# Groups of four matrices, 32-bit transposes and row-shifting copies in a batched matrix product

## The chip, the cores and the metric

The kernel runs on one NeuronCore of a Trainium2 chip. A core has a matrix engine (TensorE, in profiles PE, with its weight loads as PEld), a vector engine (VectorE, DVE), a scalar engine (ScalarE, ACT), a general engine (GpSimd, POOL) and a synchronisation engine (SyncE, SP), which here only issues transfers. Sixteen DMA engines move data between the device memory and SBUF, the on-chip memory of 128 partitions. PSUM is the small memory into which TensorE writes. Each engine works through its own instructions in order and waits on semaphores for the others. The metric is the device time of one execution, in microseconds.

## The reference

```python
b1, b2, m, k, n = 8, 16, 256, 512, 384
# x: (8, 16, 256, 512) float32, weight: (8, 16, 512, 384) float32
def reference(x, weight):
    return np.matmul(x, weight).astype(np.float32)
```

These are 128 independent products of a 256 x 512 matrix with a 512 x 384 matrix. All inputs and outputs are fp32; 168 MB are read and 50 MB written.

## The kernel before

TensorE contracts over partitions, so both operands must have the index k on the partitions. The weights have it there when they are loaded: partition kp holds the four rows k = 4 kp + ko (ko from 0 to 3) of one matrix, 6 KB in one run. x has its rows on the partitions and must be transposed on the chip.

The work is done in groups of two matrices (63 groups), and at the end two groups of one. For a pair, `load_x` (L58, its transfer issued at L60) loads 512 rows of x, four neighbouring rows to a partition (R = 4), so that each partition reads one run of 8 KB. `load_w` (L65, transfer L67) loads each weight matrix by itself.

`transpose_x` (L70) casts x to bf16 on DVE (L77). Then TensorE transposes: for each of the four rows of a partition and each ko, the 128 x 128 block of the columns ko, ko + 4, ... is transposed against an identity (L82), eight blocks to a PSUM tile `pt` of bf16, and DVE copies the tile into `x_t` (L86). The weights are cast to bf16 on DVE (L110).

Since 64 partitions of x belong to the first matrix of the pair and 64 to the second, the output of a matmul (L125) is only 64 rows wide: it takes 64 columns of `x_t` as its stationary operand and 384 columns of the weights as moving operand, and writes partitions 0 to 63 or 64 to 127 of a PSUM tile `po`. Four matmuls (ko) accumulate one result; those of the two matrices alternate. Each `po` holds two rows per partition, and ACT copies it into `out_sb` (L132), 128 partitions x 768 elements. The output has four neighbouring rows to a partition, as x has, so the store (L95) writes runs of 6 KB.

All transfers are issued by SyncE, in the order of the program: the x of a pair, its two weight matrices, then the store of an earlier pair. A store is held back until more than LAG = 4 are waiting. Buffers: `x_pool` 3, `w_pool` 6, `xb_pool` and `xt_pool` 2, `wb_pool` 4, `out_pool` 7, `psum_t` 2 and `psum_o` 3. The tile framework places the waits: a load waits until the cast that read its buffer is over, and a copy into a buffer waits until its last store is over. It also has at most eight transfers under way: each waits for the eighth before it. The instructions of one engine are put into an order by the framework's scheduler, which need not be that of the source.

Of the kernel before, what the change touches and what calls it, by code (L numbers as in the profile page):

```python
# [1 line left out]

# [5 lines left out]


@with_exitstack
def kernel(
    ctx: ExitStack,
    tc: tile.TileContext,
    x: bass.AP,
    weight: bass.AP,
    out: bass.AP,
):
    nc = tc.nc
    P = 128  # L20

    b1, b2, M, K = x.shape
    _, _, _, N = weight.shape
    B = b1 * b2
    KO = K // P

    x_rows = x.rearrange("b1 b2 m k -> (b1 b2 m) k")
    o_rows = out.rearrange("b1 b2 m n -> (b1 b2 m) n")
    w_flat = weight.rearrange("b1 b2 k n -> (b1 b2) k n")

    fp32 = mybir.dt.float32
    bf16 = mybir.dt.bfloat16

    GX = 2
    CX = P // GX
    R = GX * M // P


    groups = [2] * ((B - GX) // 2) + [1] * GX

    LAG = 4

    const = ctx.enter_context(tc.tile_pool(name="const", bufs=1))
    x_pool = ctx.enter_context(tc.tile_pool(name="x_pool", bufs=3))
    xb_pool = ctx.enter_context(tc.tile_pool(name="xb_pool", bufs=2))
    xt_pool = ctx.enter_context(tc.tile_pool(name="xt_pool", bufs=2))
    w_pool = ctx.enter_context(tc.tile_pool(name="w_pool", bufs=6))
    wb_pool = ctx.enter_context(tc.tile_pool(name="wb_pool", bufs=4))  # L50
    out_pool = ctx.enter_context(tc.tile_pool(name="out_pool", bufs=LAG + 3))
    psum_t = ctx.enter_context(tc.tile_pool(name="psum_t", bufs=2, space=bass.MemoryType.PSUM))
    psum_o = ctx.enter_context(tc.tile_pool(name="psum_o", bufs=3, space=bass.MemoryType.PSUM))

    identity = const.tile([P, P], bf16)
    make_identity(nc, identity)

    def load_x(b):  # L58
        x_sb = x_pool.tile([P, R, K], fp32, name="x_sb")
        nc.sync.dma_start(  # L60
            x_sb[:], x_rows[b * M : (b + GX) * M].rearrange("(p r) k -> p r k", r=R)
        )
        return x_sb

    def load_w(b):  # L65
        w_sb = w_pool.tile([P, KO, N], fp32, name="w_sb")
        nc.sync.dma_start(w_sb[:], w_flat[b].rearrange("(kp ko) n -> kp ko n", ko=KO))  # L67
        return w_sb

    def transpose_x(x_sb, RG):  # L70


        H = R // RG
        x_bf = xb_pool.tile([P, R, K], bf16, name="x_bf")
        x_t = xt_pool.tile([P, RG, KO, P, H], bf16, name="x_t")
        for r0 in range(0, R, 4):
            nc.vector.tensor_copy(out=x_bf[:, r0 : r0 + 4], in_=x_sb[:, r0 : r0 + 4])  # L77
            for r in range(r0, r0 + 4, 2):
                pt = psum_t.tile([P, 2, KO, P], bf16, name="pt")
                for rr in range(2):  # L80
                    for ko in range(KO):
                        nc.tensor.transpose(  # L82
                            pt[:, rr, ko, :], x_bf[:, r + rr, ko::KO], identity
                        )
                j = r % RG
                nc.vector.tensor_copy(  # L86
                    out=x_t[:, j : j + 2, :, :, r // RG], in_=pt[:]
                )
        return x_t

    waiting = []

    def store(queue):
        dram, out_sb = waiting.pop(0)
        queue.dma_start(out=dram, in_=out_sb)  # L95

    b = 0
    for n, G in enumerate(groups):
        last = n == len(groups) - 1
        C = P // G  # L100
        RG = G * M // P
        if b % GX == 0:
            x_sb = load_x(b)
        w_sb = [load_w(b + i) for i in range(G)]
        if b % GX == 0:
            x_t = transpose_x(x_sb, RG)
        w_bf = []
        for i in range(G):
            t = wb_pool.tile([P, KO, N], bf16, name="w_bf")
            nc.vector.tensor_copy(out=t[:], in_=w_sb[i][:])  # L110
            w_bf.append(t)
        if last:

            while waiting:
                store(nc.sync)

        out_full = out_pool.tile([P, 2 * M // P, N], fp32, name="out_sb")
        out_sb = out_full[:, :RG]
        for r in range(0, RG, 2):
            po = psum_o.tile([P, 2, 512], fp32, name="po")  # L120
            for rr in range(2):
                for ko in range(KO):
                    for i in range(G):
                        c0 = (b % GX + i) * CX
                        nc.tensor.matmul(  # L125
                            po[i * C : (i + 1) * C, rr, :N],
                            x_t[:, r + rr, ko, c0 : c0 + CX, :],
                            w_bf[i][:, ko, :],
                            start=(ko == 0),
                            stop=(ko == KO - 1),  # L130
                        )
            nc.scalar.copy(out=out_sb[:, r : r + 2, :], in_=po[:, :, :N])  # L132
        waiting.append(
            (
                o_rows[b * M : (b + G) * M].rearrange("(p r) n -> p r n", r=RG),
                out_sb,
            )
        )
        if len(waiting) > LAG or last:
            store(nc.sync)  # L140
        b += G


# [1 line left out]
_INS = ['x', 'weight']  # L145
_OUTS = [((8, 16, 256, 384), 'float32')]


# [23 lines left out]
```

## Time and profile before

| | |
|---|---|
| median of 3 runs | 526.35 us (526.27 to 526.38) |
| profiled execution | 526.34 us, of which its span is 524.1 us |
| HBM read, written | 167.77 MB, 50.33 MB |
| mean rate of the DMA | 417 GB/s |
| mean granted TensorE clock | 0.87 |
| w loads / x loads / stores, median from issue to landing | 16.0 us each |

The span runs from the first to the last recorded event of one execution; the execution's own time is 2.2 us longer. Busy times are sums over an engine's instructions. In the lines on the instruction groups, the numbers after the bar are the total busy time in us and the mean duration of one instruction in ns, and after the second bar the idle time just ahead of these instructions with what ended most of it. In the view of waits, the numbers are the total in us, the count and the longest. In the timeline a line gives the start, the length, the engine, the source line, the operation and the number of instructions merged into it.

### The profile page before, as it was taken

The page shows a single profiled execution, that of the slowest core. Times are in us where ns is not written, and L with a number is a line of the kernel's source. Part 1 is how long each engine was busy: PE and PEld are TensorE (multiplying, and loading weights), DVE is VectorE, ACT ScalarE, POOL GpSimd, SP SyncE. Part 2 cuts the span into 40 slices and gives each one's busy share as a digit, 9 for nine tenths or more (in the row PEclk, how much of TensorE's full clock was granted, in tenths as well). Part 3 has the DMA queues.
Part 4 walks back from the last instruction along what each step waited for, and adds up shares of the span by engine and source line. Part 5 has one row for each costly group of instructions (what it writes and reads, how often), then busy time and mean ns, then how long its engine had stood idle before and what let it go on. Part 6 is the DMA issues. An engine that isn't in the chain of part 4 may idle for free.

```text
span 524.1 us, 7422 instructions
## 1 busy us (share of the span) xinstructions
PE 339.3 (65%) x3056; PEld 231.8 (44%) x3056; DVE 273.4 (52%) x320; ACT 103.8 (20%) x129; POOL 0.7 (0%) x6
## 2 busy tenths in 40 slices
PE   4666758558576665675857657567666586556664
PEld 2444435345444443443534435444344354344442
DVE  4565464564554645546456455564554645645543
ACT  0222122121121121212212112212121121121221
POOL 0000000000000000000000000000000000000000
PEclk9989797986978889979798887988788879898888
DMA  8999999999999999999999999999999999999996
GB/s 347 418 413 423 422 424 420 424 424 419 426 420 423 423 419 425 422 424 422 424 424 423 421 425 423 425 422 423 425 423 424 423 424 425 423 422 425 423 425 272
DMA packets 37041, 218.59 MB, mean 417 GB/s; under 512 B 4112, under 2 KB 4112, under 8 KB 28816
## 3 DMA queue, kind: packets, MB, share of 16 engines
q1 hardware_dynamic: 37008, 218.12, 99.9%
q8 instruction: 24, 0.39, 0.3%
q14 instruction: 9, 0.07, 0.0%
HBM read 167.77 MB, written 50.33 MB: 416 GB/s over the span
## 4 chain that ended last, share of the span: by engine, by line
DMA 97%; PE 1%; DVE 1%; issue 0%; ACT 0%; SPq 0%; ACTq 0%; DVEq 0%
DMA x_sb<-in_x_dram 94%; DMA w_sb<-in_weight_dram 3%; PE po L125 1%; DVE x_t L86 0%; DVE x_bf L77 0%; DVE w_bf L110 0%; ACT out_sb L132 0%; PE pt L82 0%; SPq L60 0%; ACTq L132 0%; DVEq L77 0%
## 5 line engine op out<-in xcount | busy, mean ns | idle before, releaser
L125 PE MATMUL po<-w_bf,x_t 128*64 128x384 bf16 (+1 forms) x2032 | 271.0, 400 | 136.3 <-DVE w_bf L110 135.9
L125 PEld LDWEIGHTS <-x_t 128*64 128x64 bf16 (+1 forms) x2032 | 171.5, 132 | 219.8 <-DVE w_bf L110 122.8
L132 ACT COPY out_sb<-po 128x768 f32<-128x768 f32 x128 | 102.5, 801 | 416.0 <-PE po L125 404.5
L77 DVE CAST x_bf<-x_sb 128x2048 bf16<-128x2048 f32 x64 | 78.5, 1227 | 182.0 <-DMA x_sb<-in_x_dram 182.0
L110 DVE CAST w_bf<-w_sb 128x1536 bf16<-128x1536 f32 x128 | 116.7, 952 | 1.9 <-DMA w_sb<-in_weight_dram 1.9
L86 DVE COPY x_t<-pt 128x1024 bf16<-128x1024 bf16 x128 | 83.6, 696 | 59.2 <-PE pt L82 59.2
L82 PE MATMUL pt<-identity,x_bf 128*128 128x128 bf16 x1024 | 70.3, 222 | 44.1 <-DVE x_bf L77 43.7
L82 PEld LDWEIGHTS <-x_bf 128*128 128x128 bf16 x1024 | 60.3, 115 | 67.7 <-DVE x_bf L77 63.5
L132 ACT ACT_TABLE_LOAD x1 | 1.3, 1283 | 0.7 <-PEq L156 0.7
masks.py:199 POOL TENSOR_SCALAR_AFFINE_SELECT identity<-identity 128x128 bf16<-128x128 bf16 x1 | 0.3, 294 | 0.1
masks.py:197 POOL MEMSET identity<- 128x128 bf16 x1 | 0.2, 205 | 0.3 <-POOLq L156 0.3
L156 POOL MEMSET const-bfloat16-1.0<- 128x1 bf16 x1 | 0.1, 102 | 0.0
L156 POOL MEMSET const-uint8-127<- 128x1 uint8 x1 | 0.1, 102 | 0.0
L156 POOL MEMSET const-float32-0.0<- 128x1 f32 x1 | 0.1, 99 | 0.2 <-issue 0.2
L156 POOL MEMSET const-float32-1.0<- 128x1 f32 x1 | 0.1, 99 | 0.0
## 6 DMA issues: line engine op xcount, KB each, us to landing
w_sb<-in_weight_dram SPq DMA_DIRECT2D x128, 768.0 KB, 16.0
x_sb<-in_x_dram SPq DMA_DIRECT2D x64, 1024.0 KB, 16.0
out_dram<-out_sb SPq DMA_DIRECT2D x63, 768.0 KB, 16.0
out_dram<-out_sb SPq DMA_DIRECT2D x2, 384.0 KB, 3.0
```

What stands on the lines that cost most here:

```text
L77: nc.vector.tensor_copy(out=x_bf[:, r0 : r0 + 4], in_=x_sb[:, r0 : r0 + 4])
L82: nc.tensor.transpose(pt[:, rr, ko, :], x_bf[:, r + rr, ko::KO], identity)
L86: nc.vector.tensor_copy(out=x_t[:, j : j + 2, :, :, r // RG], in_=pt[:])
L110: nc.vector.tensor_copy(out=t[:], in_=w_sb[i][:])
L125: nc.tensor.matmul(po[i * C : (i + 1) * C, rr, :N], x_t[:, r + rr, ko, c0 : c0 + CX, :], w_bf[i][:, ko, :], start=(ko == 0), stop=(ko == K ...
L132: nc.scalar.copy(out=out_sb[:, r : r + 2, :], in_=po[:, :, :N])
L156: nc = _bacc.Bacc("TRN2", target_bir_lowering=False, num_devices=1)
```

## The change

Groups of four matrices take the place of pairs. Each partition now holds eight neighbouring rows of x (R = 8, runs of 16 KB) and eight of the output (runs of 12 KB); a matrix fills only 32 partitions of either.

The transposes work on 32-bit words: two neighbouring bf16 values of x, the columns 2c and 2c + 1, are taken as one fp32 word, so that one transpose moves what two did. The identity is fp32. DVE's copy (L85 of the new kernel) reads the tile as bf16 pairs and writes `x_t` so that, for each matrix i, the 32 partitions of four rows stand side by side: the stationary operand of a matmul is 128 wide and belongs to one matrix alone. The even and the odd value of each pair are picked by a step of two.

A matmul (L117) then yields 128 output rows of one matrix: row group g of the result (32 partitions) holds the rows r = g and g + 4 of that matrix's 32 partitions. The output layout wants matrix i on the partitions 32 i to 32 i + 31. So four copies (L127), of 32 partitions x 768 elements each, move the row groups g to those partitions. For g = i, where source and destination have the same partitions, DVE makes the copy, for the other three ACT. In the last group each matrix is stored by itself.

LAG goes from 4 to 2; `x_pool` from 3 to 2, `w_pool` from 6 to 8, `out_pool` from 7 to 4 (each buffer of x and of the output being twice as large).

```diff
-    GX = 2
-    CX = P // GX
-    R = GX * M // P
+    G = 4
+    C = P // G
+    R = G * M // P
+    J = R // G
-    groups = [2] * ((B - GX) // 2) + [1] * GX
-    LAG = 4
+    LAG = 2
-    identity = const.tile([P, P], bf16)
+    identity = const.tile([P, P], fp32)
...
-        x_t = xt_pool.tile([P, RG, KO, P, H], bf16, name="x_t")
+        x_t = xt_pool.tile([P, J, KO // 2, G, G, C, 2], bf16, name="x_t")
+        words = x_bf[:].bitcast(fp32)
         for r0 in range(0, R, 4):
             nc.vector.tensor_copy(out=x_bf[:, r0 : r0 + 4], in_=x_sb[:, r0 : r0 + 4])
             for r in range(r0, r0 + 4, 2):
-                pt = psum_t.tile([P, 2, KO, P], bf16, name="pt")
+                pt = psum_t.tile([P, 2, KO // 2, P], fp32, name="pt")
                 for rr in range(2):
-                    for ko in range(KO):
+                    for h in range(KO // 2):
                         nc.tensor.transpose(
-                            pt[:, rr, ko, :], x_bf[:, r + rr, ko::KO], identity
+                            pt[:, rr, h, :], words[:, r + rr, h :: KO // 2], identity
                         )
-                j = r % RG
+                j, g = divmod(r, G)
                 nc.vector.tensor_copy(
-                    out=x_t[:, j : j + 2, :, :, r // RG], in_=pt[:]
+                    out=x_t[:, j, :, :, g : g + 2].rearrange(
+                        "k h i g c e -> k g (h i) (c e)"
+                    ),
+                    in_=pt[:].bitcast(bf16).rearrange(
+                        "k g h (i ce) -> k g (h i) ce", i=G
+                    ),
                 )
...
+    for b in range(0, B, G):
+        last = b == B - G
+        x_sb = load_x(b)
+        w_sb = [load_w(b + i) for i in range(G)]
         if last:
             while waiting:
-                store(nc.sync)
...
+                store()
+        x_t = transpose_x(x_sb)
+        out_sb = out_pool.tile([P, R, N], fp32, name="out_sb")
+        for i in range(G):
+            w_bf = wb_pool.tile([P, KO, N], bf16, name="w_bf")
+            nc.vector.tensor_copy(out=w_bf[:], in_=w_sb[i][:])
+            po = psum_o.tile([P, J, 512], fp32, name="po")
+            for j in range(J):
                 for ko in range(KO):
-                    for i in range(G):
-                        c0 = (b % GX + i) * CX
-                        nc.tensor.matmul(
-                            po[i * C : (i + 1) * C, rr, :N],
-                            x_t[:, r + rr, ko, c0 : c0 + CX, :],
-                            w_bf[i][:, ko, :],
-                            start=(ko == 0),
-                            stop=(ko == KO - 1),
-                        )
-            nc.scalar.copy(out=out_sb[:, r : r + 2, :], in_=po[:, :, :N])
+                    nc.tensor.matmul(
+                        po[:, j, :N],
+                        x_t[:, j, ko // 2, i, :, :, ko % 2].rearrange("k g c -> k (g c)"),
+                        w_bf[:, ko, :],
+                        start=(ko == 0),
+                        stop=(ko == KO - 1),
+                    )
+            mine = slice(i * C, (i + 1) * C)
+            for g in range(G):
+                copy = nc.vector.tensor_copy if g == i else nc.scalar.copy
+                copy(out=out_sb[mine, g::G, :], in_=po[g * C : (g + 1) * C, :, :N])
+            if last:
+                waiting.append((o_rows[(b + i) * M : (b + i + 1) * M].rearrange(
+                    "(p r) n -> p r n", r=R), out_sb[mine]))
+                store()
+        if not last:
+            waiting.append(
+                (o_rows[b * M : (b + G) * M].rearrange("(p r) n -> p r n", r=R), out_sb[:])
+            )
+            if len(waiting) > LAG:
+                store()
```

The new line numbers that the prediction uses: L59 x load, L66 w load, L76 cast of x, L81 transposes, L85 copy into `x_t`, L99 store, L113 cast of w, L117 matmuls, L127 out copies.

More of the change, by code (lines that the diff above doesn't have):

```diff
@@ L32 @@
     bf16 = mybir.dt.bfloat16
-    GX = 2
-    CX = P // GX
-    R = GX * M // P
-    groups = [2] * ((B - GX) // 2) + [1] * GX
-    LAG = 4
+    G = 4
[3 more added lines that the diff above has]
+    LAG = 2
     const = ctx.enter_context(tc.tile_pool(name="const", bufs=1))
-    x_pool = ctx.enter_context(tc.tile_pool(name="x_pool", bufs=3))
+    x_pool = ctx.enter_context(tc.tile_pool(name="x_pool", bufs=2))
     xb_pool = ctx.enter_context(tc.tile_pool(name="xb_pool", bufs=2))
     xt_pool = ctx.enter_context(tc.tile_pool(name="xt_pool", bufs=2))
-    w_pool = ctx.enter_context(tc.tile_pool(name="w_pool", bufs=6))
+    w_pool = ctx.enter_context(tc.tile_pool(name="w_pool", bufs=8))
     wb_pool = ctx.enter_context(tc.tile_pool(name="wb_pool", bufs=4))
-    out_pool = ctx.enter_context(tc.tile_pool(name="out_pool", bufs=LAG + 3))
+    out_pool = ctx.enter_context(tc.tile_pool(name="out_pool", bufs=4))
     psum_t = ctx.enter_context(tc.tile_pool(name="psum_t", bufs=2, space=bass.MemoryType.PSUM))
     psum_o = ctx.enter_context(tc.tile_pool(name="psum_o", bufs=3, space=bass.MemoryType.PSUM))
-    identity = const.tile([P, P], bf16)
+    identity = const.tile([P, P], fp32)
     make_identity(nc, identity)
@@ L60, in load_x @@
         nc.sync.dma_start(
-            x_sb[:], x_rows[b * M : (b + GX) * M].rearrange("(p r) k -> p r k", r=R)
+            x_sb[:], x_rows[b * M : (b + G) * M].rearrange("(p r) k -> p r k", r=R)
         )
@@ L68, in load_w, with transpose_x @@
         return w_sb
-    def transpose_x(x_sb, RG):
-        H = R // RG
+    def transpose_x(x_sb):
         x_bf = xb_pool.tile([P, R, K], bf16, name="x_bf")
-        x_t = xt_pool.tile([P, RG, KO, P, H], bf16, name="x_t")
+        x_t = xt_pool.tile([P, J, KO // 2, G, G, C, 2], bf16, name="x_t")
+        words = x_bf[:].bitcast(fp32)
         for r0 in range(0, R, 4):
@@ L91, with store @@
     waiting = []
-    def store(queue):
+    def store():
         dram, out_sb = waiting.pop(0)
[L95 to L103, printed above, removed]
-        w_sb = [load_w(b + i) for i in range(G)]
-        if b % GX == 0:
-            x_t = transpose_x(x_sb, RG)
-        w_bf = []
-        for i in range(G):
-            t = wb_pool.tile([P, KO, N], bf16, name="w_bf")
-            nc.vector.tensor_copy(out=t[:], in_=w_sb[i][:])
-            w_bf.append(t)
+        nc.sync.dma_start(out=dram, in_=out_sb)
@@ L112 @@
+    for b in range(0, B, G):
+        last = b == B - G
+        x_sb = load_x(b)
+        w_sb = [load_w(b + i) for i in range(G)]
         if last:
             while waiting:
-                store(nc.sync)
[L117 to L121, printed above, removed]
-                for ko in range(KO):
-                    for i in range(G):
-                        c0 = (b % GX + i) * CX
-                        nc.tensor.matmul(
-                            po[i * C : (i + 1) * C, rr, :N],
-                            x_t[:, r + rr, ko, c0 : c0 + CX, :],
-                            w_bf[i][:, ko, :],
-                            start=(ko == 0),
-                            stop=(ko == KO - 1),
-                        )
-            nc.scalar.copy(out=out_sb[:, r : r + 2, :], in_=po[:, :, :N])
@@ L133 @@
[L133 to L136, printed above, removed]
-            )
[L138 to L141, printed above, removed]
+                store()
[6 more added lines that the diff above has]
+            for j in range(J):
+                for ko in range(KO):
+                    nc.tensor.matmul(
[13 more added lines that the diff above has]
+                store()
```

## The prediction

> **What bounds the kernel now.** I read the page from the top: busy shares, DMA, the chain that ended last, the groups; then SyncE's waits, then the timeline.
>
> ```profile
> span 524.1 us, 7422 instructions
> ...
> PE 339.3 (65%) x3056; PEld 231.8 (44%) x3056; DVE 273.4 (52%) x320; ACT 103.8 (20%) x129; POOL 0.7 (0%) x6
> ...
> DMA  8999999999999999999999999999999999999996
> ...
> q1 hardware_dynamic: 37008, 218.12, 99.9%
> ...
> DMA 97%; PE 1%; DVE 1%; issue 0%; ACT 0%; SPq 0%; ACTq 0%; DVEq 0%
> ...
> L132 ACT COPY out_sb<-po 128x768 f32<-128x768 f32 x128 | 102.5, 801 | 416.0 <-PE po L125 404.5
> L77 DVE CAST x_bf<-x_sb 128x2048 bf16<-128x2048 f32 x64 | 78.5, 1227 | 182.0 <-DMA x_sb<-in_x_dram 182.0
> L110 DVE CAST w_bf<-w_sb 128x1536 bf16<-128x1536 f32 x128 | 116.7, 952 | 1.9 <-DMA w_sb<-in_weight_dram 1.9
> L86 DVE COPY x_t<-pt 128x1024 bf16<-128x1024 bf16 x128 | 83.6, 696 | 59.2 <-PE pt L82 59.2
> L82 PE MATMUL pt<-identity,x_bf 128*128 128x128 bf16 x1024 | 70.3, 222 | 44.1 <-DVE x_bf L77 43.7
> ```
>
> The 16 DMA engines are full from the second slice to the last but one; the chain is 97% transfers, and DVE's largest idle time (182 us) waits for x to land. The last five lines are my prices. SyncE's queue, below, waits for earlier transfers and for ACT only 14.6 us in all.
>
> ```profile
> SPq L67 <- DMA w_sb<-in_weight_dram: 175.8, 118, 2.9
> ...
> SPq L95 <- ACT out_sb L132: 14.6, 4, 7.5
> ```
>
> The chain in order of time moves in pieces of 16.0 us, each two pairs of matrices: 2 x (1 MB x + 1.5 MB w + 0.75 MB out) = 6.82 MB in 16.04 us, 424 GB/s. So four matrices have a **budget of 16.04 us**: a new order is hidden below it, and above it the engines set the time. The timeline of the start shows what an engine does when nothing hinders it:
>
> ```profile
> 10.57 4.42 PE L125 MATMUL po<-w_bf,x_t 128*64 128x384 bf16 x30 [0.34 <-DVE w_bf L110]
> ...
> 16.80 1.82 DVE L110 CAST w_bf<-w_sb 128x1536 bf16<-128x1536 f32 x2
> ...
> 22.05 1.29 DVE L86 COPY x_t<-pt 128x1024 bf16<-128x1024 bf16 x2 [2.29 <-PE pt L82]
> ...
> 25.12 2.76 PE L125 MATMUL po<-w_bf,x_t 128*64 128x384 bf16 x30 [0.35 <-DVE w_bf L110]
> 27.82 1.08 PE L82 MATMUL pt<-identity,x_bf 128*128 128x128 bf16 x16
> ```
>
> Two DVE operations back to back take 0.08 to 0.10 us less than two single ones. Thirty half-width matmuls are 15 pairs side by side: 0.184 us a pair at the full clock, 0.295 where the clock is low. Sixteen transposes take 1.08 us, 0.068 each.
>
> **What the Trainium skill says.** (1) "DMA: Bandwidth & Descriptors", section Specifications, puts the fabric ceiling at 435 GB/s; the trace's 424 is 97.5% of it, so little is to be had from longer runs. (2) "ScalarE: Activation LUTs", section What ACT_TABLE_LOAD costs, prices an ACT operation with immediates at 186 ns + 0.833 ns per element and says that neighbours overlap by about 93 ns; for 768 elements that is 826, the trace has 801. No two ACT copies stand back to back here, so the overlap isn't shown; I take a spacing of 0.71. (3) "VectorE: DVE Perf Modes", section The perf-mode tier table, has fp32 out of PSUM at one element a cycle, so 768 elements cost what L110's 1536 cost at two: 0.95 us for a DVE out copy, an estimate. (4) "TensorE: Matmul & The Clock Gate", Part 1: an idle window of 3.4 us halves the clock; Terms: the transpose mode saves fp32 its fourfold cost. The granted clock here is 0.87 on average; the trace has no fp32 transpose.
>
> **The change, part by part.**
>
> *Transfers.* Data packets per four matrices fall from 64 to 48 per DMA engine (w stays 32, x 16 to 8, out 16 to 8), completion packets from 8 to 6. Taking all that separates 16.04 us from 6.82 MB at 435 GB/s (15.67) as packet cost gives 0.37/72 = 5 ns each (estimate); 18 fewer save 0.09 us of 16.04, over 32 groups 3 us. Bounds: 0 and 6 us. It counts only if transfers remain the bound.
>
> *PE.* Transposes halve in number (16 a group), at an unknown price: 0.068 us as now at best, four times the low clock's 0.107 = 0.43 at worst; I take 0.14, since fp32 weights may load more slowly. Matmuls become 32 of full width, each like a pair now. PE works about 5 of 19 us with a long pause, so I expect the low clock part of the time: 0.26 each, between 0.184 and 0.295.
>
> *DVE and ACT by sums.* DVE per group: 2 x 1.227 + 4 x 0.952 + 4 x 0.696 + 4 x 0.95 = 12.8 us. ACT: 12 x 0.80 = 9.6. Each alone fits in 16.04. This is the trap.
>
> *The order.* From group 4 on, DVE's compiled order (X cast of x, W cast of w, t copy of x_t, O out copy) is X X W0 t t W1 t t W2 O0 O1 W3 O2 O3, then the next group's X. Written (matrix, row group), ACT's is (1,0) (0,1) (0,2) (0,3) (1,2) (1,3) (2,0) (2,1) (3,0) (3,1) (2,3) (3,2). The out copies of one matrix write interleaved rows of one tile, L127, and wait for each other: O1 for ACT's (1,0), O2 for (2,1), O3 for (3,2), **ACT's last**; (0,1), (1,2), (2,3) wait for O0, O1, O2. Behind O3 in DVE's queue is the next group's X, on which its transposes, matmuls and ACT's next copy depend. So ACT's twelve copies overlap nothing of the next group's front: a serial loop. For SyncE, the loads for two groups on wait only for casts and stay early.
>
> *One group timed*, from the start of X, in us, with 0.05 from a release to a start (as L77 to L82 at the trace's end): X ends 1.23 and 2.37, W0 3.24, t 3.85 and 4.45, W1 5.32, t 5.94 and 6.53, W2 7.40. PE: eight transposes 1.28 to 2.4; four more after each t, to 5.05; then sixteen matmuls at 0.26 for matrices 0 and 1 (L117's order alternates their halves), to 9.25; with 0.3 for the pipeline (a matmul lasts 400 ns on the page, far more than its pace) matrix 0 is ready at 8.5, matrix 1 at 9.55. ACT starts (1,0) at 9.6. O0 is over by 9.5, O1 by 11.4, W3 by 12.3, matrix 3's matmuls (from 12.55, when (0,3) frees its PSUM tile) by 15.0, before (3,0) at 15.3: ACT never pauses. Twelve copies: 11 x 0.71 + 0.80 = 8.6, to 18.2. O3: 18.25 to 19.2. **The loop takes 19.2 us, against 16.04.**
>
> *Sum.* First X when 2 MB of x have landed: now 1 MB lands at 5.64, one more MB at 424 GB/s is 2.5, so 8.1. Then 32 x 19.2 = 614.4. In the first three groups the order puts the next X before O3, beside ACT's tail: about 2 us each, -6. End: the last store, now 3.0 us for 384 KB, and closing, 3.5 from the end of the last copy to the span's end. 8.1 + 614.4 - 6 + 3.5 = 620 span; the profiled execution took 526.34 for a span of 524.1, so 2.2 more: **622 us**. The shown runs' median (526.35) is that of the profiled execution.
>
> *Bounds of the loop.* Fast matmuls (0.184) put matrix 1 at 8.3: -1.2. ACT spacing 0.64 (elements alone): -0.8; no overlap: +1.0. Low clock throughout: +0.6. Transposes at 0.43: t waits, the sixteen matmuls start at about 8.1, +3.0. If the split x_t copies (2x8x64) lose the two-a-cycle rate, 0.55 each (L77 less L110 is 0.275 for 512 elements at that rate, so 1024 would cost 1.10 in place of 0.55), some of it under PE: +1 to +2. So 17.2 to about 24.
>
> **Rivals.** (a) *DMA remains the bound*: for it speak the sums (12.8 and 9.6 under 16.04) and a loading queue two groups ahead; against it the serial loop. It decides where the loop is under 16.04, 3.2 us less than I find; even all low bounds give 17.2, so several prices would have to be wrong. Then 526.34 - 3 = 523: faster. (b) *A shorter loop*, 16.3 to 18.0: warm PE and a quick ACT; 14 - 6 us of ends plus 32 loops: 530 to 584. (c) *A longer loop*, over 21.5, from fp32 transposes in four passes or slow x_t copies: at 23, 32 x 23 + 8 = 744. (d) *The waits don't act as read*, and X overlaps ACT's tail in every group: the loop loses about 2 us, 17.2: 558, within (b)'s span.
>
> **Numbers.** Forecast (loop 18.0 to 21.5: 584 to 696) 0.68; (b) with (d) 0.14; (c) 0.13; (a) 0.04; near no change 0.01. Range 580 to 695. Faster by over 0.2% (what this kernel's measurement can tell) 0.04, within 0.01, slower 0.95.
>
> **What would show it.** Right: DMA digits fall to 8 with queue share near 84%; the chain goes through ACT L127, DVE L127, L76 and L85; out copies on DVE idle about 6 us a group, most of it for ACT, while ACT has one pause of some 10 us a group, released by PE. ACT copies 0.80 us at spacing 0.71; DVE out copies 0.95; 16 transposes in 2.2 us. Wrong: DMA still at 99.9% and X idle before x lands (a); or X starting while ACT still copies the group before (d).

## The result, and the profile after

The changed kernel takes 663.74 us (median of 4 runs, 662.7 to 665.35) against 526.37 us (526.27 to 526.95): a ratio of 1.261, 95% interval 1.2581 to 1.2639. Its profiled execution took 664.31 us for a span of 662.5. The forecast was 622 us with a range of 580 to 695.

First the same lines of the page as before: the busy times, the DMA's slices, its main queue, and the groups that the prediction priced.

```profile
span 662.5 us, 4583 instructions
...
PE 333.9 (50%) x1536; PEld 214.9 (32%) x1536; DVE 393.9 (59%) x448; ACT 304.7 (46%) x385; POOL 0.7 (0%) x6
...
DMA  8999999878878789787797877987879878789324
...
q1 hardware_dynamic: 27696, 218.12, 82.0%
...
L127 ACT COPY out_sb<-po 32x768 f32<-32x768 f32 x384 | 303.4, 790 | 351.8 <-issue 302.3
L127 DVE COPY out_sb<-po 32x768 f32<-32x768 f32 x128 | 122.1, 954 | 252.6 <-ACT out_sb L127 207.1
L81 PE MATMUL pt<-identity,x_bf 128*128 128x128 f32 x512 | 126.5, 427 | 253.1 <-DVE x_bf L76 228.9
...
L85 DVE COPY x_t<-pt 128x1024 bf16<-128x1024 bf16 x128 | 85.3, 687 | 1.3
L76 DVE CAST x_bf<-x_sb 128x2048 bf16<-128x2048 f32 x64 | 75.6, 1223 | 9.6 <-DMA x_sb<-in_x_dram 8.6
```

The queue's packets fall from 37008 to 27696 at the same 218.12 MB, but the DMA is full only in the first slices. No engine is busy for more than 59% of the span: nothing is short of capacity, and the time goes into waiting. DVE's casts of x, which waited 182 us for x to land, now wait 8.6 us for it, and that is the first load. In their place stand three idle times that form a ring: DVE's out copies wait 207 us for ACT, TensorE's transposes wait 229 us for DVE's casts of x, and ACT is idle for 352 us. Most of ACT's pause carries the word "issue", which means that the profile shows no releaser for it; in the first four groups the same pause is put down to TensorE's matmuls. The page's chain of what ended last passes over such a pause as "issue" and covers only the last 27 us, so the ring has to be read from the timeline.

ACT alone, three groups (the window ends inside the third):

```profile
258.43 9.69 ACT L127 COPY out_sb<-po 32x768 f32<-32x768 f32 x12 [10.79 <-issue]
278.91 9.69 ACT L127 COPY out_sb<-po 32x768 f32<-32x768 f32 x12 [10.79 <-issue]
299.39 0.79 ACT L127 COPY out_sb<-po 32x768 f32<-32x768 f32 x1 [10.79 <-issue]
```

Twelve copies in 9.69 us, a pause of 10.79 us, and again: 20.48 us per group of four. What lies in the pause, from the timeline of all engines:

```profile
299.39 9.68 ACT L127 COPY out_sb<-po 32x768 f32<-32x768 f32 x12 [10.79 <-issue]
...
305.87 0.95 DVE L127 COPY out_sb<-po 32x768 f32<-32x768 f32 x1 [3.71 <-ACT out_sb L127]
309.11 0.96 DVE L127 COPY out_sb<-po 32x768 f32<-32x768 f32 x1 [2.29 <-ACT out_sb L127]
...
310.10 2.36 DVE L76 CAST x_bf<-x_sb 128x2048 bf16<-128x2048 f32 x2
...
311.38 1.98 PE L81 MATMUL pt<-identity,x_bf 128*128 128x128 f32 x8 [7.27 <-DVE x_bf L76]
...
314.11 1.98 PE L81 MATMUL pt<-identity,x_bf 128*128 128x128 f32 x8 [0.74 <-DVE x_t L85]
...
315.88 5.20 PE L117 MATMUL po<-w_bf,x_t 128*128 128x384 bf16 x24
...
319.87 2.41 ACT L127 COPY out_sb<-po 32x768 f32<-32x768 f32 x3 [10.79 <-issue]
```

ACT ends its twelfth copy at 299.39 + 9.68 = 309.07. Only then does DVE make its last out copy (309.11), and only after that the casts of the next group's x (310.10). That x had landed long before: its load was issued at 271.53, and loads of x land 8.9 us after issue (median). Transposes, matmuls and ACT's next copy follow in a row. While ACT makes the last of its copies, no engine works on the next group; only its loads have been made.

### The profile page after: what moved, and what is told of

It reads as the page before. It is cut to its first block, busy times and chain, and to the rows that moved or that the text cites. A ratio compares the mean times of both kernels' runs of the same rounds, so it can differ in the third digit from the quotient of the medians.

```text
span 662.5 us, 4583 instructions
## 1 busy us (share of the span) xinstructions
PE 333.9 (50%) x1536; PEld 214.9 (32%) x1536; DVE 393.9 (59%) x448; ACT 304.7 (46%) x385; POOL 0.7 (0%) x6
## 3 DMA queue, kind: packets, MB, share of 16 engines
q1 hardware_dynamic: 27696, 218.12, 82.0%
## 5 line engine op out<-in xcount | busy, mean ns | idle before, releaser
L127 ACT COPY out_sb<-po 32x768 f32<-32x768 f32 x384 | 303.4, 790 | 351.8 <-issue 302.3
L127 DVE COPY out_sb<-po 32x768 f32<-32x768 f32 x128 | 122.1, 954 | 252.6 <-ACT out_sb L127 207.1
L81 PE MATMUL pt<-identity,x_bf 128*128 128x128 f32 x512 | 126.5, 427 | 253.1 <-DVE x_bf L76 228.9
L117 PE MATMUL po<-w_bf,x_t 128*128 128x384 bf16 x1024 | 213.9, 371 | 65.2 <-ACT out_sb L127 65.2
L81 PEld LDWEIGHTS pt<-identity,x_bf 128*128 128x128 f32 x512 | 100.9, 223 | 277.9 <-DVE x_bf L76 230.9
L117 PEld LDWEIGHTS <-x_t 128*128 128x128 bf16 x1024 | 114.5, 112 | 159.0 <-issue 107.8
L113 DVE CAST w_bf<-w_sb 128x1536 bf16<-128x1536 f32 x128 | 121.8, 953 | 0.9
L85 DVE COPY x_t<-pt 128x1024 bf16<-128x1024 bf16 x128 | 85.3, 687 | 1.3
L76 DVE CAST x_bf<-x_sb 128x2048 bf16<-128x2048 f32 x64 | 75.6, 1223 | 9.6 <-DMA x_sb<-in_x_dram 8.6
```

What stands on the lines that cost most here:

```text
L81: nc.tensor.transpose(pt[:, rr, h, :], words[:, r + rr, h :: KO // 2], identity)
L85: nc.vector.tensor_copy(out=x_t[:, j, :, :, g : g + 2].rearrange("k h i g c e -> k g (h i) (c e)"), in_=pt[:].bitcast(bf16).rearrange("k g ...
L113: nc.vector.tensor_copy(out=w_bf[:], in_=w_sb[i][:])
L117: nc.tensor.matmul(po[:, j, :N], x_t[:, j, ko // 2, i, :, :, ko % 2].rearrange("k g c -> k (g c)"), w_bf[:, ko, :], start=(ko == 0), stop= ...
L127: copy(out=out_sb[mine, g::G, :], in_=po[g * C : (g + 1) * C, :, :N])
```

## The experiments

Two theories stood against the serial ring: that the out copies are simply too much work for ACT, and that the loads come too late (two buffers for x, eight for w; SyncE's queue did wait 213 us for casts of w). All ratios below are to the kernel before, measured beside each run (526.45 us).

### The same copies, shared out by matrix, and all of them on ACT

```diff
-                copy = nc.vector.tensor_copy if g == i else nc.scalar.copy
+                copy = nc.vector.tensor_copy if i == 0 else nc.scalar.copy
```

> The changed kernel, but DVE makes all four out copies of matrix 0 and ACT all twelve of matrices 1 to 3: the same number of copies on each engine (4 and 12), none of which waits for the other engine any more inside a matrix. Serial-loop theory: DVE's next cast of x no longer stands behind ACT's last copy, so the four-matrix period falls from 20.5 to the DMA's 16 us and the time to about 523 us (520 to 528). Amount-of-work theory (the copies and ACT's 0.8 us each are simply too much): same counts, so still 650 to 664 us. Late-loads theory (two x buffers and eight w buffers are too few): unchanged, about 660 us.

Measured: 528.82 us, 1.0035 of the kernel before (1.0021 to 1.0049). The second kernel has `copy = nc.scalar.copy` for all sixteen:

> The changed kernel with all sixteen out copies on ACT. Serial-loop theory: DVE waits for ACT nowhere; ACT needs 16 x 0.807 = 12.9 us a group, under 16, so the DMA bounds: about 523 us. Amount-of-work theory: ACT has a third more to do, so slower than the changed kernel, 700 us or more. Late-loads theory: unchanged, about 660 us.

Measured: 530.86 us, 1.0079 (1.0063 to 1.0094). The first keeps the counts of 4 and 12 and takes 135 us off; the second gives ACT a third more work and takes off 133. So it is not the amount of work. Nor is it TensorE's clock, which was granted at 0.87 in the kernel before and at 0.76 in the changed one: the first of these two has 0.77. DVE waits for ACT's out copies nowhere in the first one, where the changed kernel has 93 such waits. The DMA queue's share is back at 99.4% and 99.1%. Both times are some us above the 523 expected for a full DMA, and the first lies just outside its range of 520 to 528. The DMA rate in the last slices of the first one falls off earlier than in the kernel before (402 and 139 GB/s against 425 and 272):

```profile
GB/s 337 423 422 424 425 425 427 420 422 425 426 432 417 421 425 424 431 421 421 424 425 430 423 424 420 423 427 430 425 418 424 427 425 431 422 419 423 426 402 139
```

What this leaves to explain is the end of the kernel; the last experiment but one takes it up.

### The same instructions in another order

The program is rewritten so that the next group's loads and its transposition stand ahead of a group's last out copies, and the framework is told to queue DVE's out copy of matrix 3 behind the next group's casts. No instruction is taken away: DVE keeps its 448 and ACT its 385. In the excerpt `issue_after` holds the copy behind the named instruction, and `behind` says for which copies.

```diff
...
+                behind = 3 <= i == g and not last
+                with tc.issue_after(marks["cast"].ins) if behind else ExitStack():
+                    copy(out=out_sb[mine, g::G, :], in_=po[g * C : (g + 1) * C, :, :N])
...
```

> The changed kernel, each instruction kept, but on DVE the last out copy of a group (matrix 3) is queued behind the two casts of the next group's x, in all groups as it already is in the first three. Serial-loop theory: the period becomes that of the first three groups, 17.4 us, so 32 x 17.4 + 8 = about 565 us. Amount-of-work and late-loads theories: unchanged, about 660 us.

Measured: 564.23 us in one run. The second kernel of the pair queues the copies of matrices 2 and 3 behind all copies into the next `x_t` (`2 <= i == g`, and the mark set at the last of those):

> As the kernel before this one in the list, but the out copies of matrices 2 and 3 on DVE are queued behind all of the next group's transposed-x copies. Serial-loop theory: the next group's front (9.8 us) now lies beside ACT's copies; DVE, PE and ACT loops are under 16 us, so the DMA bounds: 522 to 530 us. If only the cross-waits' count mattered (they are all still there, some longer): about 660 us.

Measured: 525.02 us, 0.9971 of the kernel before (0.9959 to 0.9982), so 0.3% under it, with the interval clear of 1. DVE in the first of the two, and then ACT in each, the first one above:

```profile
316.03 2.36 DVE L78 CAST x_bf<-x_sb 128x2048 bf16<-128x2048 f32 x2
318.42 0.96 DVE L138 COPY out_sb<-po 32x768 f32<-32x768 f32 x1
```

```profile
308.56 9.69 ACT L138 COPY out_sb<-po 32x768 f32<-32x768 f32 x12 [7.38 <-issue]
325.63 9.69 ACT L138 COPY out_sb<-po 32x768 f32<-32x768 f32 x12 [7.38 <-issue]
```

```profile
312.56 0.79 ACT L138 COPY out_sb<-po 32x768 f32<-32x768 f32 x1 [5.13 <-DVE out_sb L138]
314.57 8.87 ACT L138 COPY out_sb<-po 32x768 f32<-32x768 f32 x11 [1.22 <-DVE out_sb L138]
328.58 0.79 ACT L138 COPY out_sb<-po 32x768 f32<-32x768 f32 x1 [5.14 <-DVE out_sb L138]
```

With two casts moved past one copy ACT's pause shrinks from 10.79 to 7.38 us and the period to 17.07. With the whole front moved, the period is 328.58 - 312.56 = 16.02 us, the DMA's, although ACT now waits for DVE twice in a group: the DMA queue's share is 100.0%, and DVE's casts of x again wait for x to land (66.7 us in all). The two kernels differ only in the place of those copies in DVE's queue, and that is worth 39 us. The step from 664 to 564 us also includes the rewriting, which wasn't run without the queueing. But the changed kernel's x was in place early, and the first experiment removed the loss without any rewriting. This shows the cause: it is the place of the next group's casts behind a copy that waits for ACT's last one, not the number of copies or of waits.

### The transposes as before

The 32-bit transposes are undone: the tile, the identity and `x_t` become bf16 again, `h` runs over four blocks, and the copy into `x_t` has runs of 32 elements.

```diff
...
-                    for h in range(KO // 2):
+                    for h in range(KO):
                         nc.tensor.transpose(
-                            pt[:, rr, h, :], words[:, r + rr, h :: KO // 2], identity
+                            pt[:, rr, h, :], x_bf[:, r + rr, h::KO], identity
...
```

> The changed kernel with the transposes as before: 32 bf16 transposes of 128x128 a group in place of 16 on 32-bit words; the copies into the transposed tile keep their size and number, and the out copies, their engines and their waits stay. Serial-loop theory with PE on the front: a block of eight 32-bit transposes took 1.98 us in the changed kernel, sixteen bf16 ones 1.08 in the kernel before, so the front of each loop can shorten by up to 0.9 us, and by half of that if the copies hide the rest: 635 to 655 us. If the 32-bit transposes were the main cause of the slowdown: 540 us or less. If PE is hidden behind DVE in the front: within 3 us of the changed kernel.

Measured: 628.94 us, 34.8 less than the changed kernel or 1.09 us per group, more than expected (635 to 655). The 32-bit transposes therefore add to the ring, but account for a quarter of the 137 us, not for most of it. The same stretch of the timeline of TensorE, from this kernel's casts of x at 313.42 on:

```profile
314.70 2.87 PE L80 MATMUL pt<-identity,x_bf 128*128 128x128 bf16 x24 [6.89 <-DVE x_bf L75]
318.02 1.01 PE L80 MATMUL pt<-identity,x_bf 128*128 128x128 bf16 x8 [0.46 <-DVE x_t L84]
318.83 4.91 PE L116 MATMUL po<-w_bf,x_t 128*128 128x384 bf16 x24
```

All 32 transposes together take about as long as the 16 did (3.88 against 3.96 us), but they wait less for their tiles, and the matmuls begin 5.41 us after the casts' start in place of 5.78. The scheduler also put the first copy into `x_t` ahead of the first cast of w, and the periods of this kernel scatter from 19.0 to 19.8 us. How the 1.09 us divide among these wasn't separated.

### More buffers for the weights

`w_pool` gets 10 buffers in place of 8.

> The changed kernel with ten weight buffers in place of eight, nothing else. Late-loads theory (the transfer queue's 213 us of waiting for casts of w is what costs the time): clearly faster, 600 us or less. Serial-loop theory: the loads are early in any case and the queue waits because it is ahead, so no change: 660 to 667 us.

Measured: 664.84 us in one run. The w loads are hardly held up by casts any more, and the queue merely waits elsewhere; SyncE's waits in this kernel:

```profile
SPq L99 <- DVE out_sb L127: 445.4, 33, 20.1
SPq L59 <- DVE x_bf L76: 53.2, 27, 2.0
...
SPq L66 <- DVE w_bf L113: 8.0, 27, 0.4
```

Its waiting for casts of w falls from 213 to 8 us and its waiting for DVE's last out copy rises from 255 to 445. A queue that runs ahead has to wait somewhere; its idle time was no sign of late loads. More buffers for x weren't tried, but the kernels that reach the DMA's pace above have two of them as well.

### The end of the kernel

The sharing by matrix, with each group's loads issued one group ahead in the program, and its transposition moved up with them:

```diff
...
+        if not last:
+            x_next = load_x(b + G)
+            w_next = [load_w(b + G + i) for i in range(G)]
...
+            if i == 1 and not last:
+                xt_next = transpose_x(x_next)
...
```

> As the first kernel run (DVE makes all copies of matrix 0, ACT the others), but each group's loads are issued one group ahead in the program, in front of the preceding group's store, as in the kernel with the front queued first. No engine waits for the other and the DMA bounds. If the 4 us between those two kernels lie in the order of loads and stores at the end: 524 to 526 us. If they lie in the copies' assignment: 528 to 530 us.

Measured: 525.07 us, 0.9971 (0.9959 to 0.9982), the same as with the front queued first. SyncE's queue after its last load of w, first as in the first experiment and then here:

```profile
492.02 31.04 SPq L99 DMA_DIRECT2D out_dram<-out_sb  x6
```

```profile
488.78 30.56 SPq L99 DMA_DIRECT2D out_dram<-out_sb  x7
```

Seven stores in place of six come behind the last load, so the last x is asked for at 474.51 in place of 477.77. DVE's order in the last two groups is the same in both. So the 4 us of the first experiment lay in the order of loads and stores: more stores are left to fill the DMA beside the last group's work (426 and 232 GB/s in the last two slices in place of 402 and 139).

### What the longer runs are worth

The kernel with the front queued first, each load of x and each store cut in two:

```diff
...
+        for r0 in range(0, R, R // 2):
+            nc.sync.dma_start(x_sb[:, r0 : r0 + R // 2], rows[:, r0 : r0 + R // 2])
...
+        for r0 in range(0, R, R // 2):
+            nc.sync.dma_start(out=dram[:, r0 : r0 + R // 2], in_=out_sb[:, r0 : r0 + R // 2])
...
```

> The kernel with the front queued first (525.0 us), but each load of x is made in two transfers of 8 KB runs and each store in two of 6 KB runs, so that the DMA has the packets of the kernel before (64 data and 8 completion packets per engine and group in place of 48 and 6), all else being equal. If longer runs are what brings this kernel under the kernel before: 526.5 to 528 us. If the length of the runs is worth nothing: 525 us.

Measured: 528.35 us (1.0037 of the kernel before, 1.0023 to 1.0051), 3.3 us more than with whole runs. The steady rate, busy times and rates over the same stretches, here two of each, first with halved and then with whole runs (the last number is GB/s):

```profile
188.00:252.00 64.00, 41.27 (x197) 23.92 (x198) 50.40 (x58) 39.38 (x50) 0.00 (x0) 0.83 1.02 422
316.00:380.00 64.00, 40.04 (x192) 23.15 (x190) 48.16 (x56) 36.96 (x48) 0.00 (x0) 0.82 1.01 422
```

```profile
188.00:252.00 64.00, 41.90 (x192) 25.56 (x190) 48.91 (x56) 37.67 (x48) 0.00 (x0) 0.79 1.01 424
316.00:380.00 64.00, 41.58 (x192) 25.88 (x190) 48.61 (x57) 37.66 (x49) 0.00 (x0) 0.79 1.01 425
```

The longer runs are worth 3 us of transfer, over 32 groups about 0.1 us each. The halved kernel also makes twice as many transfers of x and of the output, and how much of the 3 us belongs to these and how much to the shorter runs wasn't separated. Only 1.4 us are left in the comparison with the kernel before: with halved runs the new structure is 1.9 us slower than the kernel before, at almost equal packets (36960 against 37008). Whether that is the price of its larger first load and of its last group wasn't tried.

## Why the prediction was right, and where its sum was off

The mechanism is the one forecast, the serial loop through DVE's queue, and it was forecast from the order of the instructions. The size came out by a sum in which one term was off, two errors nearly cancelled, and the range had room for the rest. The busy sums (12.8 and 9.6 us predicted, 393.9 / 32 = 12.3 and 9.5 measured) did fit the budget of 16.04 us, and did not matter. Rival (a), a DMA that remains the bound, fell with the DMA share of 82%; but its price for packets, 3 us, is about what the halved runs measured, where packets and transfers changed together. Rival (d) fell with the timeline. (b) and (c), a shorter and a longer loop, did not come about.

The sum against the profiled execution, in us:

| term | predicted | measured | from |
|---|---|---|---|
| first cast of x | 8.1 | 8.6 | DVE's wait for the first load |
| front: start of the casts to ACT's first copy | 9.6 | 9.77 | 319.87 - 310.10 |
| ACT's twelve copies | 8.6 | 9.68 | timeline |
| last DVE copy and return | 1.0 | 1.03 | 310.10 - 309.07 |
| loop | 19.2 | 20.48 | their sum |
| groups with the casts ahead of the last copy | -6 | -5.8 | starts at 8.63, 26.36, 43.82 us |
| end | 3.5 | 4.3 | 662.5 - 658.2 |
| outside the span | 2.2 | 1.8 | 664.31 - 662.5 |
| total | 622 | 664.3 | 8.6 + 32 x 20.48 - 5.8 + 4.3 + 1.8 |

**The term that was mis-sized is ACT's spacing.** I took the overlap of neighbouring operations from the Trainium skill ("ScalarE: Activation LUTs", section What ACT_TABLE_LOAD costs: about 93 ns) and set 0.71 us a copy. The copies last 0.79 us and twelve take 9.68, 0.81 apart: no overlap at all, and the measurement decides. That is 1.1 us of each loop, 35 of the 42 us missed. The bound kept for that case, +1.0, was right; the choice was not.

**The front came out right by luck, from two errors that nearly cancel.** The 32-bit transposes take 0.247 us each (eight in 1.98), not 0.14, which delays the matmuls to 5.78 us after the casts' start in place of 5.05. From there to ACT's first copy it took 3.99 us (319.87 - 315.88) in place of the 4.55 that the sum allows. The matmuls began 0.32 us apart, at a granted clock of 0.55 over their first 2.56 us, and then ran at 1.00: 24 in 5.20, 0.217 each in place of 0.26. The remaining 0.17 us a loop makes 5 us more.

**The saving by the order of the first groups was right in sum, wrong in its parts.** Only two of the transitions have the casts ahead of the last copy, not three, and they save 2.75 and 3.0 us, not 2. Where every group had that order (the kernel of 564.23 us), the period fell by 3.41.

**DVE as forecast:** its out copies take 954 ns (0.95), and the copies into `x_t` in runs of 64 keep their rate (687 ns), so that bound wasn't needed. The upper end of the loop's bounds was added up too low: 19.2 with all four upper terms is 24.8 to 25.8, not about 24.

**SyncE's queue was read in part.** The loads are early, as forecast, but they don't wait only for casts: the queue's largest wait, 254.9 us, is a store's wait for DVE's last out copy, and the loads stand behind it. It cost nothing here, since x and w had landed before their casts: these waited for loads 8.6 us in all. Of the signs named, ACT's one pause is there (10.79 us), but its release by TensorE is shown in the first four groups only, and the page's chain is too short to show the loop.

## What to carry to other kernels

Compare busy sums with the budget of a stage, but then follow the in-order queues once around. A copy that waits for another engine's last instruction delays everything queued behind it, and when the next stage's first instruction is there, two engines that each fit the budget add up instead of overlapping. Two engines that write interleaved parts of one tile may be made to wait for each other; sharing the work by whole partition blocks costs the same and removes these waits. And where such a ring is found, moving the next stage's start ahead of the waiting copy can be worth more than making a step of the ring faster: here 139 us, down to the DMA's pace, against 35 for the one step that was tried.

## What the runs showed of the hardware that I had not expected

Back-to-back ACT copies out of PSUM don't overlap in these runs: 0.79 us each, 0.81 apart. A 128 x 128 transpose of 32-bit words took 0.247 us here, twice what a bf16 transpose took in the same place (24 in 2.87 us, 0.12 each), both at a granted clock of 0.50. So moving pairs halved the instructions here and not TensorE's time; at a higher clock it wasn't measured. Halved against whole runs (18 packets per engine and group apart) gives 422 against 424.5 GB/s over 6.82 MB, about 0.1 us; put down to packets alone, that is an estimate of 5 ns a packet.
